# Rotary scores of a latent attention: the low keys' product over 128 partitions instead of 64

## Chip, cores and metric

One core of one Trainium2 chip runs the whole program. The metric is the device time of one execution in microseconds (us). Before the change three runs took 2120.97, 2120.96 and 2120.81 us; the median is 2120.96 us.

## What is computed

A trunk of two layers over 256 tokens of 2048 features. Each layer is a token mixer and a gated channel mixer, with a norm before and after each. The change lies in the second layer's mixer, an attention with low-rank queries, keys and values and a rotary part that all 16 heads share on the side of the keys. Cut from the reference:

```python
q = (rms_norm(c_q, q_a_norm) @ w_uq).reshape(bsz, seq, C_HEADS, C_NOPE_DIM + C_ROPE_DIM)     # 16 heads, 128 + 64
q = jnp.concatenate([q[..., :C_NOPE_DIM], apply_rope(q[..., C_NOPE_DIM:], cos, sin)], axis=-1)
kv = (rms_norm(c_kv, kv_a_norm) @ w_ukv).reshape(bsz, seq, C_HEADS, C_NOPE_DIM + C_V_DIM)
k_nope, v = kv[..., :C_NOPE_DIM], kv[..., C_NOPE_DIM:]
k_rope = apply_rope(k_r[:, :, None, :], cos, sin)                                             # one, for all heads
k = jnp.concatenate([k_nope, jnp.broadcast_to(k_rope, (bsz, seq, C_HEADS, C_ROPE_DIM))], axis=-1)
o = dense_block_attention(q[:, :, :, None, :], k, v, (C_NOPE_DIM + C_ROPE_DIM) ** -0.5)
return o @ w_out
```

So a score is a product over 128 features plus a product over 64 rotary features.

## The kernel before

Every operand of a product is kept as two float32r parts, high and low, and a product is high high + high low + low high. Weights come in chunks of 128 x 1024 numbers: SyncE loads `raw` (L103), ScalarE casts it to `whi` (L117), VectorE subtracts to get `wlo` (L118), three buffers each. TensorE works through the chunks one after another in the two layers' order: mixer 0, channel mixer 0, mixer 1, channel mixer 1. Between two chunks a `tick` lets generators make one step each; softmaxes, transposes and evacuations are such steps and are so woven into the stream of products. The order on each engine is fixed when the program is built.

`mixer1` first makes the two latent tiles `cq` and `ckv` and the rotary keys `kr`. For each of 8 pairs of heads it then takes a chunk for the queries (`proj_pair`, L172 to L174), one for the keys, one for the values, and for every second pair one for the rotary queries, whose parts are turned and copied to `qr` (L833). A head is then one call of `attend`:

- its two blocks of 128 queries each get a sum of products over 256 keys in PSUM, all issued by L471, **five products a block**. Three are over the 128 plain features (`qk`). The fourth and fifth are the rotary ones. `qr` holds the 64 high features of a head on partitions 0 to 63 and the 64 low ones on partitions 64 to 127; `kr[:, 0, :]` holds the high keys twice, on either half. The fourth product, over all 128 partitions, so gives high high and low high at once. The fifth is high high features by low keys: `qr[0:64]` by `kr[0:64, 1, :]`, over 64 partitions.
- VectorE takes the maxima (L480, L482), ScalarE the exponentials (L487) and the high weights (L492), VectorE the low ones (L493). Some ticks later TensorE transposes them (L252), ScalarE copies these to `pT` (L506), and TensorE multiplies by the values.

Heads come in twos, so the products of L471 stand in 8 runs of 20 (the first run has a few others between).

`kr` is made once, by `evac_kr`: two transposes of 64 partitions (L803), the rotary, four transposes back, and one ScalarE copy out of PSUM (L816, 128 x 512), which fills `kr[:, 1, :]` on all 128 partitions too, with the low keys twice.

Ahead of `mixer1` stands the end of the first layer's channel mixer (`out_proj`): the second half of the tokens' products end, ScalarE takes their square sums (L292) and a root (L382), VectorE makes the norm's factor of it (`postv` L383, `postu` L385 and L386, `postr` L387) and adds to the residual x (L391), TensorE transposes x (L413), and its parts (L527, L528) are what mixer 1's first products (L172) wait for.

The lines that say it:

```python
ps = self.psum("at").rearrange("p (i k) -> p i k", i=2)
for i in range(2):
    pairs = scores(i)
    for n, (l, r) in enumerate(pairs):
        self.tc.keep_in_program_order(
            nc.tensor.matmul(ps[:, i, :], l, r, start=n == 0, stop=n == len(pairs) - 1))      # L471
```

Of the kernel before, what the change touches and what calls it, by code (L numbers as in the profile page):

```python
# [9 lines left out]
F32 = mybir.dt.float32  # L10
# [16 lines left out]
HOLD = 3        # chunks of weights kept at the end of an output projection, see proj_tok  # L27
LAGS = 3, 2, 1  # ticks from a softmax to its transposes, from these to the values, from a rotary to its transposes

# columns of the packed vectors  # L30
# [7 lines left out]
class Model:  # L38
    """All products are of operands in two float32r parts, high and low: high high + high low + low high.

    A sublayer's input x is kept as parts of x times the pre-norm's gain, features on the partitions; the norm's
    factor of a token goes in where the products leave PSUM (or into the factors of the scores).
    """
# [14 lines left out]
    def now(self, gen, after=()):  # L58
        """A generator that steps at every tick, once those of `after` have ended."""
        self.soon.append((gen, tuple(after)))  # L60
        return gen

    def later(self, gen, after=()):
        """A generator of the queue, of which a few run at a time."""
        self.bg.append((gen, tuple(after)))
        return gen
# [55 lines left out]
    def behind(self, instructions):  # L122
        """A block whose instructions are issued after these, on their engines."""
        stack = ExitStack()
        for ins in instructions:
            stack.enter_context(self.tc.issue_after(ins.ins))
        return stack

    def weights(self, upto=None):
        """The parts of the next chunk; those after it, before `upto`, get split and loaded."""  # L130
        i = self.at
        if upto is None:
            upto = i + (2 if self.lead else 3)
            self.follow()
        for j in range(i, upto):
            self._split(j)
        for j in range(upto, i + 6):
            self._load(j) if j < upto + 4 else None
        self.at += 1
        return self.made.pop(i)  # L140

    def follow(self):
        """Ahead of a chunk: the tiles of x that it meets, if they aren't there yet."""
        if self.lead and not next(self.lead, False):
            self.lead, self.gate = None, ()

# [4 lines left out]
    def warm(self, n):  # L151
        """Products of zeros, for the array's clock to stay up while its next operands get made."""
        ps = self.psum("acc")
        for _ in range(n):
            self.tc.keep_in_program_order(
                self.nc.tensor.matmul(ps[:, :T], self.zeros[:, :P], self.zeros, start=True, stop=True))

    def acc(self, n):
        """n PSUM banks for sums; evacuations that would still hold them come first."""
        while self.held and sum(k for _, k in self.held) + n > 4:  # L160
            self.finish(self.held.popleft()[0])
        return [self.psum("acc") for _ in range(n)]
# [6 lines left out]
    def mm3(self, ps, lh, ll, rh, rl, start, stop):  # L169
        """ps (+)= l.T @ r of operands in two parts."""  # L170
        mm = self.nc.tensor.matmul
        mm(ps, lh, rh, start=start, stop=False)  # L172
        mm(ps, lh, rl, start=False, stop=False)  # L173
        mm(ps, ll, rh, start=False, stop=stop)  # L174

    def proj_t(self, nk, x, tag):
        """[512 outputs] x [256 tokens], outputs on the partitions: 4 PSUM tiles, their halves to be added."""
        mm = self.nc.tensor.matmul
        out = [self.psum(tag) for _ in range(4)]
        for c in range(nk // 2):  # L180
            hi, lo = self.weights()
            for i in range(4):
                for kk in range(2):
                    k = 2 * c + kk
                    s = slice(kk * 512 + i * P, kk * 512 + (i + 1) * P)
                    mm(out[i], hi[:, s], x(k), start=k == 0, stop=False)  # L186
                    mm(out[i][:, :T], lo[:, s], x(k)[:, :T], start=False, stop=k == nk - 1)  # L187
            self.tick()
        return out

    def proj_tok(self, nk, x, order=None, before={}, hold=0):
        """[256 tokens] x [512 outputs], tokens on the partitions: 2 PSUM tiles.

        The last `hold` chunks are kept for the first half of the tokens to be done before the second.
        """
        out = self.acc(2)
# [26 lines left out]
    def proj_small(self, x, n, nk):  # L223
        """[256 tokens] x [n outputs] of one chunk of weights [128, nk * n], tokens on the partitions."""
# [12 lines left out]
    def proj_pair(self, x):  # L237
        """Two heads of [128 outputs] x [256 tokens] of one chunk, outputs on the partitions."""
# [11 lines left out]
    def turn(self, out, x):  # L250
        """out[f, t] = x[t, f] of a float32r block."""
        self.tc.keep_in_program_order(self.nc.tensor.transpose(out, x, self.ident_r))  # L252

    def joined(self, sp, out, ps):
        """The sum of a proj_t tile's halves."""
        b = sp.tile([P, T], F32, tag="half", name="half", bufs=2)
        self.nc.scalar.copy(b, ps[:, T:])  # L257
        self.nc.vector.tensor_tensor(out=out, in0=ps[:, :T], in1=b, op=ALU.add)
        return out

# [4 lines left out]
    def heron(self, s, v, r):  # L265
        """r = 1 / sqrt(v) from the table's root s, by a step of Heron's rule: 2 s / (s s + v)."""
# [6 lines left out]
    def rstd_over(self, ss, r, n, dim):  # L273
        """Factors of a norm of r * x, r a row's factor, from x's square sums ss [128, 2, n], times r."""
# [19 lines left out]
    def table(self, f, x):  # L294
        """Have the table of f loaded ahead of its use, once x [128, 1] is there."""
        self.nc.scalar.activation(self.spare, x, f)

    def pre_norm(self, sp=None):
        """self.r [128 tokens, 2], and on request self.rb [128, 256 tokens] alike on all partitions; a generator."""
# [29 lines left out]
    def split(self, k, src, pre):  # L329
        """Feature tile k of x, transposed, times the gain as two float32r parts."""  # L330
# [11 lines left out]
    def out_proj(self, nk, parts, post, pre, order=None, before={}):  # L342
        """x += post-norm of the output projection; then x's parts for the next product, or x to DRAM.

        The first half of the tokens ends ahead of the second, so that its part of the norm and of the sum lies
        under products; the parts of x come in pairs of feature tiles, of which the next sublayer's first chunks
        of weights ask (see follow).
        """
# [109 lines left out]
    def attend(self, scores, sc, mask, v, v_gen, put, sp):  # L458
        """scores(i): the (lhsT, rhs) of query block i; sc [128 queries, 2]: factors of the scores, or a number;
        v(j): the parts of [128 keys, 128], there once the generator in v_gen has ended; a generator."""  # L460
# [64 lines left out]
    def parted_by(self, hi, lo, x, r):  # L525
        """The parts of x * r."""
# [4 lines left out]
    def mixed(self, sp):  # L531
        """The attention's outputs in parts, feature tiles."""
# [5 lines left out]
    def turned(self, sp, ps, n, block, tab, put, scale=None):  # L538
        """Rotary of n heads, tokens on the partitions, neighbouring blocks of `block` turned against each other,
        times scale(t) of the rows or scale(t, i) of a head's; the parts, transposed, go to put(i); a generator."""  # L540
# [37 lines left out]
    def first_x(self, sp):  # L578
        """The first parts of x, a pair of tiles ahead of each chunk of weights."""
# [154 lines left out]
    def mixer1(self, pre):  # L734
        nc, tc, a = self.nc, self.tc, self.a
        with tc.tile_pool(name="mix1", bufs=1) as sp:
# [8 lines left out]
            kr = sp.tile([P, 2, T], F32R, name="kr")  # L745

# [23 lines left out]
            def rope(y, z, v, n):  # L770
                """y = rotary of v, [128, 2, n heads, 64]; z is room."""
# [22 lines left out]
            def evac_kr(ps):  # L794
                """The shared rotary keys: high parts on either half of the partitions; low parts too."""
# [20 lines left out]
                nc.scalar.copy(kr, pt.bitcast(F32))  # L816
# [24 lines left out]
            for p in range(8):  # L841
# [21 lines left out]
                def head(h, qk=qk, v=v, qr=qr, v_gen=v_gen):  # L863
                    i = h % 2

                    def scores(b):
# [3 lines left out]
                                (qr[0][:, h % 4, bs], kr[:, 0, :]), (qr[0][0:64, h % 4, bs], kr[0:64, 1, :])]  # L870
# [83 lines left out]
def _tiled(w, n=512):  # L954
    """[K, N] -> [N / n, K * n / 131072, 128, 1024]: a chunk, 1024 / n blocks of rows, is a contiguous piece."""
# [6 lines left out]
def _rope(pos, dim):  # L962
    """Cosines and signed sines, [positions, dim] each, of halves turned against each other."""
# [52 lines left out]
```

## Time and profile before

| | |
|---|---|
| median of three runs | 2120.96 us |
| span of the profiled execution | 2119.2 us |
| TensorE (PE) busy | 2106.1 us, 99% of the span |
| VectorE (DVE) busy | 1331.3 us, 63% |
| ScalarE (ACT) busy | 1140.5 us, 54% |
| chain that ended last | PE 98%, DVE 1%, ACT 1% |
| granted TensorE clock, mean | 0.999 |

The profiled execution's span, from its first to its last instruction, is 2119.2 us, 1.8 us under the median of the runs. A share over the whole span says little about one stage; mixer 1's attention lies between about 1159 and 1291 us, and the rows below are of that stage and of the border ahead of it. PE is counted busy from a product's start to its modelled end, and products overlap, so a pause between two products shows in the distance between their starts and not in the busy time.

### The profile page before, as it was taken

What the parts mean: (1) busy time and instruction counts of PE and PEld (TensorE: products, weight loads), DVE (VectorE), ACT (ScalarE), POOL (GpSimd) and SP (SyncE); (2) the same over time, 40 slices, a digit from 0 to 9 for tenths busy, and PEclk for the clock granted to TensorE, in tenths of its full rate; (3) what the DMA queues carried; (4) which work ended last, traced back from release to release, by engine and by line L of the source; (5) the groups of instructions that cost most, each with busy time, mean ns of one, the idle gap of its engine ahead of it and who ended that gap; (6) DMA issues with size and microseconds to landing.
All of it is one profiled execution on the core that took longest, in us unless ns stands there. A gap on an engine that the chain in (4) does not pass through costs nothing.

```text
span 2119.2 us, 29704 instructions
## 1 busy us (share of the span) xinstructions
PE 2106.1 (99%) x11317; PEld 1787.4 (84%) x11317; DVE 1331.3 (63%) x2004; ACT 1140.5 (54%) x1814; POOL 0.2 (0%) x4
## 2 busy tenths in 40 slices
PE   9999999999999999999999999999999999999998
PEld 7888878888888888888888998788888888888886
DVE  6776657767667666444466764576676766754444
ACT  6766546555555555334355765465555555543433
POOL 0000000000000000000000000000000000000000
PEclk9999999999999999999999999999999999999999
DMA  8545565666666666666655335566666666666664
GB/s 312 170 138 159 167 182 176 182 195 188 191 192 183 195 189 190 191 191 193 194 182 164 102 108 155 169 194 191 190 187 195 184 196 190 185 193 194 194 189 149
DMA packets 108718, 385.99 MB, mean 182 GB/s; under 512 B 12064, under 2 KB 12576, under 8 KB 108576
## 3 DMA queue, kind: packets, MB, share of 16 engines
q1 hardware_dynamic: 108288, 383.83, 60.1%
q8 instruction: 88, 1.44, 0.3%
q14 instruction: 54, 0.44, 0.1%
q10 hardware_dynamic: 288, 0.28, 0.0%
HBM read 381.96 MB, written 2.10 MB: 181 GB/s over the span
## 4 chain that ended last, share of the span: by engine, by line
PE 98%; DVE 1%; ACT 1%; DMA 0%; issue 0%; DVEq 0%; SPq 0%
PE ps L186 31%; PE ps L174 16%; PE ps L172 16%; PE ps L173 16%; PE ps L187 15%; PE ps L471 2%; PE ps L252 2%; DVE x L391 0%; PE ps L413 0%; DMA raw<-in_w_in 0%; ACT whi L117 0%; ACT junk L292 0%; PE ps L789 0%; DVE xhl L528 0%; PE ps L790 0%
## 5 line engine op out<-in xcount | busy, mean ns | idle before, releaser
L118 DVE TENSOR_TENSOR wlo<-raw,whi 128x1024 fp32r<-128x1024 f32 (+1 forms) x710 | 867.1, 1222 | 698.3 <-ACT whi L117 697.6
L117 ACT CAST whi<-raw 128x1024 fp32r<-128x1024 f32 (+1 forms) x710 | 743.8, 1048 | 775.9 <-PE ps L174 421.6
L186 PE MATMUL ps<-xhl,whi 128*128 128x512 f32 x2816 | 978.6, 394 | 1.0 <-DVE xhl L528 1.0
L187 PE MATMUL ps<-xhl,wlo 128*128 128x256 f32 x2816 | 779.1, 277 | 0.0
L186 PEld LDWEIGHTS ps<-xhl,whi 128*128 128x128 f32 x2816 | 527.6, 188 | 123.1 <-DVE xhl L528 2.1
L187 PEld LDWEIGHTS ps<-xhl,wlo 128*128 128x128 f32 x2816 | 528.9, 188 | 1.0 <-DVE wlo L118 0.5
L174 PE MATMUL ps<-whi,gl 128*128 128x512 f32 x704 | 280.9, 399 | 0.0
L173 PE MATMUL ps<-wlo,gh 128*128 128x512 f32 x704 | 277.4, 394 | 0.0
L172 PE MATMUL ps<-whi,gh 128*128 128x512 f32 x704 | 276.0, 392 | 0.0
L173 PEld LDWEIGHTS ps<-wlo,gh 128*128 128x128 f32 x704 | 132.2, 188 | 34.5
L172 PEld LDWEIGHTS ps<-whi,gh 128*128 128x128 f32 x704 | 132.2, 188 | 31.4
L174 PEld LDWEIGHTS ps<-whi,gl 128*128 128x128 f32 x704 | 132.2, 188 | 30.3
L172 PE MATMUL ps<-whi,xhl 128*128 128x512 f32 x352 | 138.5, 395 | 1.5 <-ACT whi L117 1.5
L173 PE MATMUL ps<-wlo,xhl 128*128 128x512 f32 x352 | 137.9, 392 | 0.0
L174 PE MATMUL ps<-whi,xhl 128*128 128x512 f32 x352 | 137.6, 392 | 0.0
L172 PE MATMUL ps<-whi,oh 128*128 128x512 f32 x256 | 101.5, 397 | 0.0
L174 PE MATMUL ps<-whi,ol 128*128 128x512 f32 x256 | 101.4, 396 | 0.0
L173 PE MATMUL ps<-wlo,oh 128*128 128x512 f32 x256 | 100.9, 394 | 0.0
L257 ACT COPY half<-ps 128x256 f32<-128x256 f32 x176 | 65.0, 369 | 45.7 <-PE ps L186 36.0
L172 PEld LDWEIGHTS ps<-whi,xhl 128*128 128x128 f32 x352 | 65.9, 188 | 15.1 <-ACT whi L117 1.7
L174 PEld LDWEIGHTS ps<-whi,xhl 128*128 128x128 f32 x352 | 66.0, 188 | 14.0
L173 PEld LDWEIGHTS ps<-wlo,xhl 128*128 128x128 f32 x352 | 66.1, 188 | 13.3 <-DVE wlo L118 0.9
(177 smaller groups left out, 1722.4 us busy)
## 6 DMA issues: line engine op xcount, KB each, us to landing
raw<-in_w_up SPq DMA_DIRECT2D x352, 512.0 KB, 4.2
raw<-in_w_down SPq DMA_DIRECT2D x176, 512.0 KB, 4.2
raw<-in_w_in SPq DMA_DIRECT2D x88, 512.0 KB, 4.0
raw<-in_w_out SPq DMA_DIRECT2D x64, 512.0 KB, 4.0
gb<-in_post SPq DMA_DIRECT2D x16, 256.0 KB, 4.2
raw<-in_w_qn SPq DMA_DIRECT2D x8, 512.0 KB, 3.6
raw<-in_w_kn SPq DMA_DIRECT2D x8, 512.0 KB, 3.5
raw<-in_w_v SPq DMA_DIRECT2D x8, 512.0 KB, 3.6
```

The costliest lines, as they stand in the source:

```text
L117: self.nc.scalar.copy(hi[:, s], raw[:, s])
L118: self.nc.vector.tensor_tensor(out=lo[:, s], in0=raw[:, s], in1=hi[:, s].bitcast(F32), op=ALU.subtract)
L172: mm(ps, lh, rh, start=start, stop=False)
L173: mm(ps, lh, rl, start=False, stop=False)
L174: mm(ps, ll, rh, start=False, stop=stop)
L186: mm(out[i], hi[:, s], x(k), start=k == 0, stop=False)
L187: mm(out[i][:, :T], lo[:, s], x(k)[:, :T], start=False, stop=k == nk - 1)
L252: self.tc.keep_in_program_order(self.nc.tensor.transpose(out, x, self.ident_r))
L257: self.nc.scalar.copy(b, ps[:, T:])
L471: nc.tensor.matmul(ps[:, i, :], l, r, start=n == 0, stop=n == len(pairs) - 1))
```

## The change

`kr[64:, 1, :]`, the second copy of the low keys, is replaced by zeros: a memset writes them once at the start of `mixer1`, and the copy out of PSUM is split in two so that it leaves them alone. The fifth product then takes `qr` and `kr` on all 128 partitions; its upper half multiplies the low features of the queries by zeros. Comments were also taken out of the file; two lines are added in all, so that lines behind the memset have a number one higher and those behind the copy two higher.

```diff
@@ mixer1
             kr = sp.tile([P, 2, T], F32R, name="kr")
+            nc.vector.memset(kr[64:, 1, :].bitcast(F32), 0.0)
...
@@ evac_kr
-                nc.scalar.copy(kr, pt.bitcast(F32))
+                nc.scalar.copy(kr[:, 0, :], pt[:, 0, :].bitcast(F32))
+                nc.scalar.copy(kr[0:64, 1, :], pt[0:64, 1, :].bitcast(F32))
...
@@ scores
-                                (qr[0][:, h % 4, bs], kr[:, 0, :]), (qr[0][0:64, h % 4, bs], kr[0:64, 1, :])]
+                                (qr[0][:, h % 4, bs], kr[:, 0, :]), (qr[0][:, h % 4, bs], kr[:, 1, :])]
```

TensorE's instructions keep their order and their waits, and so do SyncE's. Two places change on the other engines. The first is VectorE at the end of the first layer's `out_proj`, in the order after the change (`postv` to `postr` are the second half of the tokens' factor, `x` is the residual, in brackets is the engine or queue waited for):

```order
L391 SCALAR_TENSOR_TENSOR x_343<-m_9425,postr,x_343 128x512
L118 TENSOR_TENSOR wlo<-raw,whi 128x1024 [waits DMAHW3_49,Activation_49]
L746 MEMSET kr 64x256 [waits PE_49]
L383 TENSOR_SCALAR postv<-posta,part 128x1 [waits Activation_49]
L385 SCALAR_TENSOR_TENSOR postu<-posts,postv 128x1 [waits DVE_49,Activation_49]
L386 RECIPROCAL postu<-postu 128x1 [waits DVE_49]
L387 TENSOR_SCALAR postr<-posts,postu 128x1 [waits DVE_49]
```

The memset is the only row that is new there; written at the start of `mixer1`, it is placed behind a split of weights and ahead of the factor. The PE instruction that it waits for is the last product of this `out_proj` (L174), since `kr` lies where a tile of the channel mixer lay.

The second place is ScalarE where `kr` is filled (`v` and `qk` are the first heads' evacuations), before:

```order
L522 CAST qk<-ps 128x2x256 [waits PE_49]
L816 CAST kr<-ps 128x512 [waits PE_49]
L117 CAST whi<-raw 128x1024 [waits DMAHW6_49,PE_49,Activation_49]
L522 CAST v<-ps 128x512
L117 CAST whi<-raw 128x1024 [waits DMAHW7_49,PE_49,Activation_49]
```

and after:

```order
L522 CAST qk<-ps 128x2x256 [waits PE_49]
L817 CAST kr<-ps 128x256 [waits PE_49]
L818 CAST kr<-ps 64x256
L117 CAST whi<-raw 128x1024 [waits DMAHW6_49,PE_49,Activation_49]
L522 CAST v<-ps 128x512
```

One copy became two, in the same place.

## Rows read from the trace of the kernel before

**Rows 1.** The page's first line of busy times, and its chain of waits by engine.

```profile
PE 2106.1 (99%) x11317; PEld 1787.4 (84%) x11317; DVE 1331.3 (63%) x2004; ACT 1140.5 (54%) x1814; POOL 0.2 (0%) x4
PE 98%; DVE 1%; ACT 1%; DMA 0%; issue 0%; DVEq 0%; SPq 0%
```

**Rows 2.** The instructions of L471 that read `qk` and `kr`: count, shortest, median and longest time in ns, first and last start in us, and forms (partitions * columns of the array, then the operand's shape). PEld is the load of the operand that stays in the array.

```profile
L471 PE MATMUL ps<-qk x96: 277/282/388, 1159.3 to 1277.4; 128*128 128x256 f32 x96
L471 PEld LDWEIGHTS ps<-kr,qr x64: 182/185/189, 1160.1 to 1277.7; 128*128 128x128 f32 x32, 64*128 64x128 f32 x32
L471 PE MATMUL ps<-kr,qr x64: 276/330/384, 1160.2 to 1277.7; 128*128 128x256 f32 x32, 64*128 64x256 f32 x32
```

**Rows 3.** The timeline of PE and of PEld over one block of scores and the start of the next, from narrow windows: start in us, time in us, engine, line, operation, form, how many were merged.

```profile
1160.71 0.62 PE L471 MATMUL ps<-qk 128*128 128x256 f32 x3
1161.06 0.19 PEld L471 LDWEIGHTS ps<-kr,qr 128*128 128x128 f32 x1
1161.17 0.28 PE L471 MATMUL ps<-kr,qr 128*128 128x256 f32 x1
1161.38 0.18 PEld L471 LDWEIGHTS ps<-kr,qr 64*128 64x128 f32 x1
1161.38 0.38 PE L471 MATMUL ps<-kr,qr 64*128 64x256 f32 x1
1161.69 0.39 PE L471 MATMUL ps<-qk 128*128 128x256 f32 x1
1161.92 0.40 PE L471 MATMUL ps<-qk 128*128 128x256 f32 x2
```

**Rows 4.** The timeline of PE over products of a chunk of weights, of the same shape (17 in a row, of which the first and the last are shown), and over the two transposes of 64 partitions in `evac_kr`.

```profile
1164.01 0.28 PE L172 MATMUL ps<-whi,ckv 128*128 128x256 f32 x1
...
1165.93 0.28 PE L173 MATMUL ps<-wlo,ckv 128*128 128x256 f32 x1
...
1145.78 0.28 PE L174 MATMUL ps<-cq,wlo 128*128 128x256 f32 x1
1145.99 0.34 PE L803 MATMUL ps<-ident,raw 64*128 64x64 f32 x2
1146.25 0.38 PE L172 MATMUL ps<-ckv,whi 128*128 128x256 f32 x1
1146.47 0.28 PE L173 MATMUL ps<-ckv,whi 128*128 128x256 f32 x1
```

**Rows 5.** The chain of waits in order of time, around the fifth run of L471: start, time, engine, tile and line, number of instructions.

```profile
1224.11 3.74 PE ps L471 x20
...
1228.16 0.12 PE ps L173
```

**Rows 6.** The timeline of DVE and ACT, and pieces of the chain of waits, at the border of the two layers. In square brackets is the idle time ahead of an instruction and what ended it.

```profile
1081.45 1.22 DVE L118 TENSOR_TENSOR wlo<-raw,whi 128x1024 fp32r<-128x1024 f32 x1
1082.62 0.21 DVE L383 TENSOR_SCALAR postv<-posta,part 128x1 f32<-128x1 f32 x1
...
1082.62 0.29 ACT L382 ACTIVATE posts<-posta,part 128x1 f32<-128x1 f32 x1
...
1082.95 0.23 DVE postu L385
...
1085.20 0.50 PE ps L172
```

**Rows 7.** The two memsets that the kernel has on DVE (groups of the page's kind: busy us, mean ns of one).

```profile
L928 DVE MEMSET zeros<- 128x128 uint32 x1 | 0.2, 165 | 0.0
L924 DVE MEMSET eps<- 128x1 f32 x1 | 0.1, 59 | 0.8 <-PEq L1008 0.8
```

**Rows 8.** The timeline of ACT at the copy to `kr` and behind it, and the summary of another copy out of PSUM, of 128 x 256 (L518).

```profile
1152.45 0.59 ACT L816 CAST kr<-ps 128x512 fp32r<-128x512 f32 x1 [1.23 <-PE ps L252]
1152.93 1.05 ACT L117 CAST whi<-raw 128x1024 fp32r<-128x1024 f32 x1
1155.62 1.05 ACT L117 CAST whi<-raw 128x1024 fp32r<-128x1024 f32 x1 [1.15 <-issue]
...
L518 ACT CAST oh<-ps x32: 349/368/423, 89.0 to 1296.3; 128x256 fp32r<-128x256 f32 x32
```

**Rows 9.** The timeline of DVE and ACT at the first two heads' softmax, and of PE where the last of their weights get transposed.

```profile
1160.97 0.69 DVE L523 TENSOR_TENSOR qk<-ps,qk 128x512 fp32r<-128x512 f32 x1 [0.23 <-ACT qk L522]
1161.80 0.69 DVE L480 TENSOR_REDUCE nm<-ps 128x2 f32<-128x512 f32 x1
1163.77 0.69 DVE L480 TENSOR_REDUCE nm<-ps 128x2 f32<-128x512 f32 x1 [1.28 <-PE ps L471]
1164.61 1.28 ACT L487 ACT_TABLE_LOAD   x1 [3.68 <-DVE nm L482]
...
1171.68 0.28 PE L173 MATMUL ps<-cq,whi 128*128 128x256 f32 x1
1171.85 0.28 PE L252 MATMUL ps<-ident_r,phl 128*128 128x128 f32 x1
```

**Rows 10.** Busy time of the engines in the stretch from the second run of L471 to the third: window, its length, then busy us and instructions of each engine, granted clock, DMA's busy share and GB/s. Under it, from the summary of L471, what PE sat idle for ahead of it: us in all, times.

```profile
1172.77:1189.63 16.86, 16.86 (x137) 15.80 (x137) 12.43 (x23) 13.04 (x30) 0.00 (x0) 1.00 0.42 125
...
  ACT pT L506: 0.7, 3
```

## Prediction

> **What bounds the kernel now.** I read the page's first lines, then L471 by itself, then single instructions, then the neighbours that could take over. The page says that TensorE is busy 99% of the span and makes up 98% of the chain that ended last [rows 1]. So a microsecond taken out of TensorE's stream counts in full, as long as what feeds it keeps up, and one added beside it counts nothing. Busy time does not show where that stream stands still, though: products overlap, so I go by the distance of their starts.
>
> The summary of L471 shows a difference of form: the products by `kr` have a median of 330 ns against 282 ns of those by `qk`, and half of them, 32, are over 64 partitions [rows 2]. The timeline of one block shows what that does [rows 3]. The fourth product, over 128 partitions, starts at 1161.17 and its load had started at 1161.06, under the products before it. The fifth, over 64, starts at 1161.38 and its load starts only then. The next block's first product, again over 128, starts at 1161.69, its second at 1161.92. So the three distances from the fourth product on are 0.21, 0.31 and 0.23 us, 0.75 us in all. Products of the same shape whose partitions stay at 128 stand (1165.93 - 1164.01) / 16 = 0.12 us apart [rows 4], three of them 0.36 us. **A block loses 0.75 - 0.36 = 0.39 us around its fifth product.**
>
> That it is the change of 64 and 128 partitions, and not the tiles `qr` and `kr`, is supported by the only other place with 64 partitions, the two transposes at L803 [rows 4]: 0.21 us from the last full product to the first of them, and 0.22 us from the first full product behind them to the next, as here, with other tiles and another operation. The fourth product reads the same two tiles as the fifth and follows its predecessor without a pause.
>
> A rule of the Trainium skill speaks against this change: in "TensorE: Matmul & The Clock Gate", section "LDWEIGHTS (loading the stationary operand)", a load's time is set by its columns, and "A 32×128 weight load takes the same time as a 128×128 weight load". The trace agrees for the load's own time, 182 to 189 ns over both forms [rows 2]. By that rule alone widening the product to 128 partitions would gain nothing, and the sum would be 2121.2 us; it is the start of the load that differs in the rows, and on that the rule says nothing. It is rival D below.
>
> **The change part by part.**
>
> *The fifth product over 128 partitions.* Each of the 32 blocks has one. The column count is unchanged, so the product itself gets no longer than a neighbour of 0.12 us. If the pauses at both borders go, 32 x 0.39 = 12.5 us. The same from a whole run: 20 products of L471 and the one behind take 1228.16 - 1224.11 = 4.05 us in the chain [rows 5], where 21 at 0.12 would take 2.52; 1.53 us a run, for 8 runs 12.2 us. The two differ by rounding; I take 12.3. It lies on the chain, in full. Its bounds: 12.5 above; below, nothing, if the pauses have another cause.
>
> *The memset.* It is not on TensorE's stream but it isn't free either. It stands on VectorE ahead of `postv`, and waits for the last product of that sublayer, which ACT's square sums wait for as well, so the wait itself adds none. But VectorE isn't idle there: the split `wlo` runs from 1081.45 for 1.22 us and `postv` follows it at once, at 1082.62 [rows 6]. The memset goes between. Its price: 165 ns for 128 columns of 4 bytes, 59 ns for one [rows 7]; for 256 columns that extends to 59 + 255 x (165 - 59) / 127 = 272 ns (an estimate from these two rows). `postv` would end at about 1082.62 + 0.27 + 0.21 = 1083.10 instead of 1082.83; `postu`, which today waits for ACT's root (1082.62 + 0.29 = 1082.91) and starts at 1082.95, would start some 0.15 to 0.2 us later. From there everything up to mixer 1's first product at 1085.20 is on the chain [rows 6]. I take **+0.2 us**; bounds 0 (the split ends earlier than it shows) and 0.3.
>
> *The split copy to `kr`.* One copy of 128x512 takes 0.59 us, the next starts 0.48 us after it [rows 8]; two of 256 columns would take some 0.37 us each [rows 8], so ACT gets 0.15 to 0.25 us more. It delays the split of weights behind it, and behind that ACT is idle for 1.15 us [rows 8], which takes it up; the first use of `kr` is at 1160.2 [rows 2], 7 us later. I put **+0.1 us** for what VectorE passes on before; bounds 0 and 0.25. Were that idle time gone, the whole 0.25 would show.
>
> *What a shorter run triggers.* Scores that end sooner let the softmax start sooner, but the transposes behind it also come sooner. In the later runs the chain is released by the scores' end, so both move. The first run is the tight one: VectorE waited 1.28 us for the second head's scores before the reduction at 1163.77, so this can move by that and by the 0.14 us that the first reduction can move up to the end of the subtraction ahead of it (1160.97 + 0.69 = 1161.66 against 1161.80) [rows 9], 1.42 of the 1.53 us. ACT, idle for 3.68 us before the table load at 1164.61, follows. PE already waits a little at the end of that softmax: the transpose at 1171.85 starts 0.17 us after the product ahead [rows 9]. So **+0.1 us** is given back there; bounds 0 and the run's whole 1.53. Late next are the transposes' copies to `pT`, for which PE idles 0.7 us in three times [rows 10]; they follow the transposes on the same engine and stay as they are.
>
> *What feeds TensorE.* The stretch from the second run to the third has ACT at 13.04 of 16.86 us and VectorE at 12.43 [rows 10]. With 1.53 us less it is 15.33 us, and ACT is at 85%, VectorE at 81%. DMA's share of 0.42 there becomes 0.46. All of them still fit.
>
> **The sum:** -12.3 + 0.2 + 0.1 + 0.1 = **-11.9 us**. Against the profiled execution, 2119.2 us of span, that is 2107.3; its median of runs lies 1.8 us above the span, so I forecast **2109.1 us**. By the bounds of the terms that are likely (gain 12.2 to 12.5, additions 0 to 2.1 us) the time lies between 2108.5 and 2110.9.
>
> **The rivals.**
>
> *A, the forecast*, 2109.1 us: 0.85.
>
> *B, one border stays.* The pause going in (0.21 - 0.12 = 0.09 us a block) could be due to the fourth and fifth product sharing the operand in the array, or to something else that the change leaves. Then 32 x 0.09 = 2.9 us stay: 2112.0 us. Against it: the first and second product of a block share theirs too. From 1160.71 to 1161.17 are three distances, 0.46 us [rows 3]; the first of them is the way out of the block before, 0.23 us as from 1161.69 to 1161.92, and leaves 0.12 us for each of the others, no pause. 0.04.
>
> *C, ACT takes over.* At 85% in the second stretch, with softmaxes that come in twos, ACT could hold the transposes back so that the first run's and one more run's gain turn into waits: 2 x 1.53 = 3.1 us back, 2112.1 us. For it: the tight transpose at 1171.85 [rows 9]. Against it: at the first run VectorE waits 1.28 us for PE, and ACT 3.68 us for VectorE [rows 9]. 0.06.
>
> *D, the slower side.* The pauses come not from the count of partitions but from a switch that stays, say of the pair of tiles. Then nothing is gained, and what decides is the memset ahead of `postv`: from the point where it ends later than ACT's root (1082.91) every part of it is on the chain, and with 0.2 us the time is 2121.2 us, above the time before. To be slower by a measurable amount it would have to take over 4 us, which the 165 ns of the other memset speak against. The rule of the Trainium skill above ends here too ("TensorE: Matmul & The Clock Gate", same section): by that rule, partitions are free. Against D: the pause at L803. 0.04.
>
> *E, the change doesn't do what it says*, for instance because the product built still reads 64 partitions: 2121.2 us with the same additions. The indices in the diff read all 128; 0.01.
>
> **How the numbers follow.** The likeliest case gives 2109.1. Its own range is 2108.5 to 2110.9; with it alone 0.85 is held, and I widen it a little, for rounding and for additions that I haven't seen, to 2108.0 to 2111.4. B to E, 0.15, lie outside. A measurement of this kernel can tell about 0.2%, 4.2 us, from no change. A, B and C are all faster by more than that: 0.95. D and E are within: 0.04 of their 0.05, and I leave 0.01 for a D whose additions cost over 4.2 us.
>
> **What would show it.** In the profile after: all 64 products by `kr` of the form 128*128, with a median near 280 ns; a run of L471 of 20 products in about 2.4 us instead of 3.74; the fifth product's load starting ahead of it, as the fourth's does. The memset stands between `wlo` and `postv` with some 0.27 us, and mixer 1's first product starts about 0.2 us later. The two copies to `kr` take some 0.7 us together. The stage from the first run to the last is shorter by about 11 us (seven runs at 1.53) in step with PE, and PE's idle time in it stays below 1 us. The forecast is wrong if pauses of over 0.05 us remain around the fifth products, if PE gets new waits for `phl` or `pT` of over 1 us, or if time changes outside 1080 to 1300 us.

## The result, and the profile after

Nine runs of each kernel were made beside each other: a median of 2109.01 us after (lowest 2108.62) and 2121.14 us before (lowest 2120.81). The ratio is 0.9938, with a 95% interval of 0.9913 to 0.9962; the two medians alone make 0.9943. The interval is wide because runs of either kernel come at two levels some 9 us apart, before 6 near 2121 and 3 near 2130, after 5 near 2108.8 and 4 near 2117.8, and the ratio takes them all in. From lowest to lowest it is -12.19 us; in the profiled executions the span went from 2119.2 to 2106.8 us, -12.4 us. The forecast was 2109.1 us, with a span of 2107.3.

The page after, busy times and chain, against [rows 1]:

```profile
PE 2093.1 (99%) x11317; PEld 1783.0 (85%) x11317; DVE 1330.9 (63%) x2005; ACT 1139.5 (54%) x1815; POOL 0.2 (0%) x4
PE 98%; DVE 1%; ACT 1%; issue 0%; DMA 0%; DVEq 0%; SPq 0%
```

The count of products is the same; PE's busy time is 13.0 us shorter, since the modelled ends of the products had covered the pauses and so counted them as busy, and PE still makes up the chain.

All instructions on the tile `kr` after (count, shortest/median/longest ns, first and last start us, forms), against [rows 2, 7, 8]:

```profile
L471 PEld LDWEIGHTS ps<-kr,qr x64: 187/188/192, 1160.5 to 1265.5; 128*128 128x128 f32 x64
L471 PE MATMUL ps<-kr,qr x64: 277/280/282, 1160.6 to 1265.6; 128*128 128x256 f32 x64
L746 DVE MEMSET kr<- x1: 272/272/272, 1082.8 to 1082.8; 64x256 f32 x1
L817 ACT CAST kr<-ps x1: 377/377/377, 1152.9 to 1152.9; 128x256 fp32r<-128x256 f32 x1
L818 ACT CAST kr<-ps x1: 368/368/368, 1153.1 to 1153.1; 64x256 fp32r<-64x256 f32 x1
```

All 64 products have one form, and their median fell from 330 to 280 ns. The memset takes the 272 ns that were worked out.

PE and its loads over a block (timeline, narrow windows), against [rows 3]: first the loads of the next block before, then the whole block after.

```profile
1161.69 0.42 PEld L471 LDWEIGHTS ps<-qk 128*128 128x128 f32 x3
```

```profile
1161.09 0.30 PEld L471 LDWEIGHTS ps<-kr,qr 128*128 128x128 f32 x2
1161.20 0.40 PE L471 MATMUL ps<-kr,qr 128*128 128x256 f32 x2
1161.32 0.31 PEld L471 LDWEIGHTS ps<-qk 128*128 128x128 f32 x2
1161.44 0.52 PE L471 MATMUL ps<-qk 128*128 128x256 f32 x3
1161.79 0.40 PE L471 MATMUL ps<-kr,qr 128*128 128x256 f32 x2
```

The fourth and fifth product now go from 1161.20 to 1161.44 and the next three from there to 1161.79, 0.12 us each. The load for the next block starts at 1161.32, ahead of its product, where it used to start with it (both at 1161.69). A whole run, from the chain of waits, against [rows 5]:

```profile
1218.15 2.36 PE ps L471 x20
```

2.36 us instead of 3.74. Comparing the start of every product in the two traces shows the whole account:

| place | PE's shift against before, us |
|---|---|
| up to 1080 us | +0.05 |
| first transposes behind the norm's factor (1084 us) | +0.50 |
| first product of the scores (1160 us) | +0.42 |
| behind the eighth run (1300 us) | -12.36 |
| from 1400 us to the end | -12.40 |

In every block the shift has three steps: 0.09 at the fifth product, 0.19 at the next and 0.11 at the one behind, 0.39 us in all. After the last run nothing moves by more than 0.07 us.

### The profile page after: what moved, and what is told of

Read it like the earlier page. It is cut to its first block, busy times and chain, and to the rows that moved or that the text cites. A ratio compares the mean times of both kernels' runs of the same rounds, so it can differ in the third digit from the quotient of the medians.

```text
span 2106.8 us, 29706 instructions
## 1 busy us (share of the span) xinstructions
PE 2093.1 (99%) x11317; PEld 1783.0 (85%) x11317; DVE 1330.9 (63%) x2005; ACT 1139.5 (54%) x1815; POOL 0.2 (0%) x4
## 4 chain that ended last, share of the span: by engine, by line
PE 98%; DVE 1%; ACT 1%; issue 0%; DMA 0%; DVEq 0%; SPq 0%
PE ps L186 31%; PE ps L174 16%; PE ps L172 16%; PE ps L173 16%; PE ps L187 15%; PE ps L252 2%; PE ps L471 2%; DVE x L391 0%; PE ps L413 0%; DMA raw<-in_w_in 0%; ACT whi L117 0%; ACT junk L292 0%; PE ps L790 0%; DVE wlo L118 0%; DVE xhl L528 0%
## 5 line engine op out<-in xcount | busy, mean ns | idle before, releaser
L186 PE MATMUL ps<-xhl,whi 128*128 128x512 f32 x2816 | 978.6, 394 | 1.0 <-DVE xhl L528 1.0
L187 PE MATMUL ps<-xhl,wlo 128*128 128x256 f32 x2816 | 779.2, 277 | 0.0
L186 PEld LDWEIGHTS ps<-xhl,whi 128*128 128x128 f32 x2816 | 527.6, 188 | 123.0 <-DVE xhl L528 2.0
L187 PEld LDWEIGHTS ps<-xhl,wlo 128*128 128x128 f32 x2816 | 528.9, 188 | 1.1 <-DVE wlo L118 0.6
L174 PE MATMUL ps<-whi,gl 128*128 128x512 f32 x704 | 280.9, 399 | 0.0
L174 PEld LDWEIGHTS ps<-whi,gl 128*128 128x128 f32 x704 | 132.2, 188 | 30.4
L174 PE MATMUL ps<-whi,xhl 128*128 128x512 f32 x352 | 137.6, 392 | 0.0
L174 PE MATMUL ps<-whi,ol 128*128 128x512 f32 x256 | 100.9, 394 | 0.0
L174 PEld LDWEIGHTS ps<-whi,xhl 128*128 128x128 f32 x352 | 66.0, 188 | 14.0
```

## The experiments

The times of each stand against runs of the kernel before that were made beside it, the starts of its products against the one trace of the kernel before. Where a profile fell on the upper level of times, only its part up to 1360 us is compared; the last section says why.

**The change once more**, without an edit.

> The changed kernel once more, as the yardstick for the others of this chip. It takes out the pauses (0.394 us a block, 32 blocks, 12.6 us) and adds the memset ahead of the norm's factor (0.44 us by the shift of the first transposes behind it). Expected span 2106.8 us, lowest run 2108.6 us, 12.2 us under the lowest run before. If the difference of 12.2 us was of the one chip, it would be off by over 1 us here.

Five runs took 2108.52, 2108.53, 2108.62, 2108.74 and 2117.54 us, against a lowest of 2120.43 before: -11.9 us. (A sixth took 6584.21 us; nothing shows why, and it is set aside.) The profiled run is the one of 2117.54, and its span is 2115.7. The difference came again within 0.3 us of the first.

**All 128 partitions without zeros.** The low keys' second copy is left where it was:

```diff
-                                (qr[0][:, h % 4, bs], kr[:, 0, :]), (qr[0][0:64, h % 4, bs], kr[0:64, 1, :])]
+                                (qr[0][:, h % 4, bs], kr[:, 0, :]), (qr[0][:, h % 4, bs], kr[:, 1, :])]
```

> The kernel before with one edit: the fifth product reads all 128 partitions of both tiles, and the upper half of the low keys stays the second copy that was there. It so adds the product of the low features and low keys, which the kernel before leaves out. No memset, no split copy. Theory (the pauses come from the borders between products over 64 and over 128 partitions; the memset costs 0.44 us on the chain at the end of the first layer): 32 products of full height, no pause, and 0.4 us less than the change: span 2106.4 us, lowest run 2108.2 us. Rival (it is the zeros that make the product quick): pauses stay or come back in part, over 2110 us. Rival (the 0.44 us is made up later by something else): 2108.6 us, as the change.

Products of `kr` in its trace (summary of the tile), and VectorE at the border of the layers (timeline), against [rows 6]:

```profile
L471 PEld LDWEIGHTS ps<-kr,qr x64: 187/188/192, 1159.8 to 1264.9; 128*128 128x128 f32 x64
L471 PE MATMUL ps<-kr,qr x64: 277/280/282, 1159.9 to 1265.0; 128*128 128x256 f32 x64
```

```profile
1081.27 1.22 DVE L118 TENSOR_TENSOR wlo<-raw,whi 128x1024 fp32r<-128x1024 f32 x1
1082.44 0.21 DVE L383 TENSOR_SCALAR postv<-posta,part 128x1 f32<-128x1 f32 x1
1082.77 0.22 DVE L385 SCALAR_TENSOR_TENSOR postu<-posts,postv 128x1 f32<-128x1 f32 x1
```

The pauses are gone without any zeros, and `postv` follows the split at once again. Between 1040 and 1360 us PE gains 12.87 us on the kernel before, the change 12.41: the additions cost the difference, 0.46 us. So the zeros are not what makes the product quick. The lowest run is 2108.09 us, as the theory had it. But 10 of its 12 runs took 2116.8 to 2118.2 us, and the median is 2116.94 (ratio 0.997, 0.9957 to 0.9982): it is no better version of the whole program as it stands.

**Half as many borders.** In the second block of a head the order of the five products is turned round, so that two products over 64 partitions follow each other:

```diff
-                        return [(qt[:, 0, bs], kt[:, 0, :]), (qt[:, 0, bs], kt[:, 1, :]), (qt[:, 1, bs], kt[:, 0, :]),
+                        pairs = [(qt[:, 0, bs], kt[:, 0, :]), (qt[:, 0, bs], kt[:, 1, :]), (qt[:, 1, bs], kt[:, 0, :]),
                                 (qr[0][:, h % 4, bs], kr[:, 0, :]), (qr[0][0:64, h % 4, bs], kr[0:64, 1, :])]
+                        return pairs if b == 0 else pairs[::-1]
```

> The kernel before, the order of the products turned round in the second block of each head: the fifth product of the first block, over 64 partitions, is followed by that of the second block, also over 64. So there are 16 pairs and 32 borders instead of 64; nothing else moves. Theory (each border between 64 and 128 partitions costs, not the product itself): the second of a pair starts about 0.12 us after the first, and 16 x 0.39 = 6.3 us go; span 2112.9 us. Rival (every product over 64 partitions pauses, wherever it stands): 2119.2 us, as before, with distances of 0.2 to 0.3 us between the two of a pair. Rival (the pause sits between the fourth product and the fifth because these two read the same operand in the array): also as before.

One run, 2114.72 us, with a span of 2112.9, just what the theory said; by its second channel mixer it lies on the lower level (346.7 ns a pair of products there, see the last section). The timeline of PE over one pair, from narrow windows (merged rows overlap; the first row of `kr` is the first block's fourth product, then the two over 64 partitions, the second block's fourth, and the three by `qk`):

```profile
1160.31 0.28 PE L471 MATMUL ps<-kr,qr 128*128 128x256 f32 x1
1160.51 0.81 PE L471 MATMUL ps<-kr,qr 64*128 64x256 f32 x3
1160.74 0.59 PE L471 MATMUL ps<-kr,qr 64*128 64x256 f32 x2
1160.94 0.38 PE L471 MATMUL ps<-kr,qr 128*128 128x256 f32 x1
1161.16 0.52 PE L471 MATMUL ps<-qk 128*128 128x256 f32 x3
```

The distances are 0.20, 0.23, 0.20 and 0.22 us, against four of 0.117: 0.39 us lost for the pair, where two products apart lost that much each. The second product over 64 partitions does not start 0.12 us after the first, as I had written, but 0.23, inside the 0.2 to 0.3 us of the rival; it is the span, 6.3 us shorter, that speaks against the rival. The four distances fit this: **each border costs 0.09 us at the first product behind it and 0.11 us at the second**, 0.19 to 0.20 us in all. Before, the product between two borders had both at once, 0.12 + 0.11 + 0.09, the 0.31 us of [rows 3]. So the rival of a pause that belongs to every product over 64 partitions falls, since there are as many of them as before and half the loss is gone. That of a pause between two products that read the same operand in the array falls too: such neighbours are as many as before, and with 128 partitions the fourth and fifth still share theirs and stand 0.12 us apart. Three or more products over 64 in a row were not run.

**96 partitions.** The kernel before, its fifth product with `0:96` in the place of `0:64`:

```diff
-                                (qr[0][:, h % 4, bs], kr[:, 0, :]), (qr[0][0:64, h % 4, bs], kr[0:64, 1, :])]
+                                (qr[0][:, h % 4, bs], kr[:, 0, :]), (qr[0][0:96, h % 4, bs], kr[0:96, 1, :])]
```

> The kernel before, the fifth product over 96 partitions instead of 64 (it adds 32 of the low features by the low keys, which the kernel before leaves out). In the built program a product over 64 partitions asks for an array of 64 x 128, one over 96 for the whole 128 x 128, as one over 128 does. Theory 1 (the pause comes with the change of the array's form, 64 x 128 against 128 x 128): no pause, span 2106.4 us. Theory 2 (the pause comes with any change of the count of partitions): pauses of 0.39 us a block stay, span 2119.2 us.

```profile
L471 PEld LDWEIGHTS ps<-kr,qr x64: 187/188/192, 1159.5 to 1264.6; 128*128 128x128 f32 x32, 96*128 96x128 f32 x32
L471 PE MATMUL ps<-kr,qr x64: 276/281/287, 1159.6 to 1264.7; 128*128 128x256 f32 x32, 96*128 96x256 f32 x32
```

In this summary of `kr`, half of the products are over 96 partitions, and the median is 281 ns. PE gains 12.80 us between 1040 and 1360 us, against 12.87 with 128. So the count of partitions may change without a pause, and theory 2 falls. Theory 1 fits: what costs is the change between the array's 64 x 128 form, which the built program asks for with 64 partitions, and its whole 128 x 128. That the program asks for the whole array with 96 is read from the program; the trace prints 96\*128. Only 64, 96 and 128 were run. (The run took 2116.68 us, its profile on the upper level.)

**The additions alone.** The change, with the fifth product over 64 partitions:

```diff
-                                (qr[0][:, h % 4, bs], kr[:, 0, :]), (qr[0][:, h % 4, bs], kr[:, 1, :])]
+                                (qr[0][:, h % 4, bs], kr[:, 0, :]), (qr[0][0:64, h % 4, bs], kr[0:64, 1, :])]
```

> The change without its gain: memset and split copy as in it, the fifth product over 64 partitions as before. Theory (the memset holds back the norm's factor by 0.44 us, the split copy costs nothing): all pauses there, TensorE 0.44 us later than before from the first transposes behind the factor on and no more than that at the first scores; span 2119.7 us. Rival (the forecast's sizes, memset 0.2 us and copy 0.1 us): 2119.5 us, with a step of 0.2 us at the border of the layers and another of 0.1 us at about 1160 us.

One run of 2121.59 us, with a span of 2119.8; by the starts of PE it is 0.55 us behind the kernel before from 1200 us to the end. 0.45 us come in one step, at the first transposes behind the factor. The other 0.13 us come between 1120 and 1200 us, in steps of 0.06 and 0.07. They could be the split copy's, but that isn't shown: the run with half as many borders has no split copy and moves by 0.05 us between 1120 and 1160 us as well, and in the change itself nothing is seen of it.

**The memset on POOL.**

```diff
-            nc.vector.memset(kr[64:, 1, :].bitcast(F32), 0.0)
+            nc.gpsimd.memset(kr[64:, 1, :].bitcast(F32), 0.0)
```

> The change with its memset on the POOL engine instead of VectorE; the same sums. Theory (the 0.44 us is the memset's place in VectorE's line, ahead of the factor): they come back, the norm's factor ends as early as before the change; span 2106.4 us, lowest run 2108.2 us, in the rhythm of products that the change's first profile shows in the second channel mixer. Rival (a memset anywhere at that time costs, since it waits for the same last product and writes beside VectorE): 2106.8 us, lowest 2108.6 us. In the other rhythm of products, which two profiles showed, either is 8.9 us longer.

POOL's timeline, then VectorE's:

```profile
1081.84 0.31 POOL L746 MEMSET kr<- 64x256 f32 x1 [1081.40 <-PE ps L174]
```

```profile
1081.37 1.22 DVE L118 TENSOR_TENSOR wlo<-raw,whi 128x1024 fp32r<-128x1024 f32 x1
1082.54 0.21 DVE L383 TENSOR_SCALAR postv<-posta,part 128x1 f32<-128x1 f32 x1
1082.86 0.22 DVE L385 SCALAR_TENSOR_TENSOR postu<-posts,postv 128x1 f32<-128x1 f32 x1
```

The same memset on another engine, where it starts a microsecond sooner, costs the factor nothing: PE gains 12.87 us between 1040 and 1360 us. Runs took 2108.22, 2108.26, 2108.44, 2117.06, 2117.24 and 2117.24 us; against the change's lowest of 2108.52 in another set of runs that is 0.3 us, which agrees with the 0.46 us but wouldn't show it by itself.

**A product of zeros in the second channel mixer.** On the version with 128 partitions and no zeros, once, ahead of the second half of the sixth group:

```diff
+                if layer == 1 and gi == 5:
+                    ps = self.psum("at")
+                    self.tc.keep_in_program_order(
+                        nc.tensor.matmul(ps[:, :T], self.zeros[:, :P], self.zeros, start=True, stop=True))
                 pv = self.proj_t(KD, x, "at")
```

> The kernel in which the fifth product also takes the low features by the low keys, with one more product, of zeros, in the second channel mixer, between the two halves of its sixth group of eleven. In two profiles the products of that mixer ran in a rhythm of three pairs, 349, 350 and 361 ns, in the others of two, 350 and 343 ns, from the same place on to the end of that stage. Theory (the rhythm is a matter of how the train of products is started, and stays until it is broken): after the extra product the rhythm can differ from that ahead of it within one run, and times between 2108.2 and 2117.0 us occur, near 2112.9 us where it changes. Rival (it is a property of the whole run, of memory or of the chip): the same rhythm ahead and behind, times at 2108.4 and 2117.2 us only.

Nine of ten runs took 2116.92 to 2118.24 us, and one 2113.04, a time that neither of the two levels has and that is near the 2112.9 of a rhythm that changes half way. The profile is of a run of 2117.13 us and has the same rhythm ahead and behind. One run supports the theory; it does not settle it.

**Another order of the channel mixers' products.** On the same version:

```diff
+                s = [slice(kk * 512 + i * P, kk * 512 + (i + 1) * P) for kk in range(2)]
                 for kk in range(2):
-                    k = 2 * c + kk
-                    s = slice(kk * 512 + i * P, kk * 512 + (i + 1) * P)
-                    mm(out[i], hi[:, s], x(k), start=k == 0, stop=False)
-                    mm(out[i][:, :T], lo[:, s], x(k)[:, :T], start=False, stop=k == nk - 1)
+                    mm(out[i], hi[:, s[kk]], x(2 * c + kk), start=c + kk == 0, stop=False)
+                for kk in range(2):
+                    mm(out[i][:, :T], lo[:, s[kk]], x(2 * c + kk)[:, :T], start=False, stop=2 * c + kk == nk - 1)
```

> The kernel in which the fifth product also takes the low features by the low keys, with another order in both channel mixers' first products: two products over 512 columns and then two over 256, where they alternated. Sums and counts are the same. Theory (the two rhythms, 346.7 and 353.3 ns a pair, come from the alternation of 512 and 256 columns): one rhythm only, runs within 1 us of each other, at about 2108.2 us if four products still take 693 ns; 22 groups of 64 pairs make each ns a pair worth 1.4 us a layer. Rival (the rhythms don't depend on the order in the pair): two levels of times again, 2108.2 and 2117.0 us.

Five runs took 2113.08 to 2113.32 us: one level, as the theory said, but 5 us above the lower one. In the second channel mixer a pair takes 348.3 ns here, against 346.7 and 353.3 in the two rhythms.

## Where the prediction was right, and which steps failed

- **Where TensorE stands still.** Right. The pause came with the change between 64 and 128 partitions; it went at both ends (rival B is out), and loads start ahead of their products again. It is not the number of partitions as such: 96 among 128 cost nothing. The array's form fits all the runs. The argument from L803 was sound.
- **The rule that a load's time does not hang on its partitions** (the Trainium skill, "TensorE: Matmul & The Clock Gate", section "LDWEIGHTS (loading the stationary operand)"). It holds here for the load's own time, 182 to 192 ns in any form. What rival D drew from it, no gain and 2121.2 us, did not come: the change of form costs 0.19 to 0.20 us a border.
- **The gain, 12.3 us. This step failed in size:** 12.87 us with nothing added, above the 12.5 that the forecast gave as its upper bound. Three distances were set against 0.12 us, read from a chunk's products; in a run of L471 a product takes 2.36 / 20 = 0.118 us, and the three steps are 0.394 us a block, 12.6 us. Of the remaining 0.25 us, 0.08 come ahead of the first scores, where the version without zeros has no edit that could act, and so are no part of the gain; the others are small steps inside the stage, whose cause was not traced.
- **The memset, 0.2 us. This step failed in size too:** it cost 0.45, above its bound of 0.3. I let the 0.27 us start where `postv` had started and gave `postu` a slack of 0.12 us. The chain of waits after shows both wrong:

```profile
1081.58 1.14 DVE wlo L118
1082.72 0.11 issue
1082.83 0.27 DVE kr L746
1083.10 0.03 issue
1083.13 0.22 DVE postv L383
1083.36 0.03 issue
1083.38 0.02 DVEq L385
1083.40 0.04 issue
1083.45 0.23 DVE postu L385
...
1085.69 0.50 PE ps L172
```

  The memset starts 0.11 us behind the split's end (0.11 also in the second trace of the change and in that of the additions alone), where `postv` had started 0.05 us ahead of it [rows 6], and `postu` starts 0.09 us after the end of `postv` in this chain, so 0.03 us of slack were left, not 0.12. 0.11 + 0.05 + 0.27 + 0.03 - 0.03 makes 0.43.
- **The split copy, 0.1 us.** The change shows none: PE's shift is +0.50 at the factor and +0.42 at the first scores. The two copies and the split behind them cost ACT some 0.06 us (0.54 us to the next start, 0.48 before [rows 8]). ACT's idle time behind takes it:

```profile
1152.86 0.38 ACT L817 CAST kr<-ps 128x256 fp32r<-128x256 f32 x1 [1.23 <-PE ps L252]
1153.13 0.37 ACT L818 CAST kr<-ps 64x256 fp32r<-64x256 f32 x1
1153.40 1.06 ACT L117 CAST whi<-raw 128x1024 fp32r<-128x1024 f32 x1
1156.03 1.06 ACT L117 CAST whi<-raw 128x1024 fp32r<-128x1024 f32 x1 [1.10 <-issue]
```

- **The first run's softmax, 0.1 us.** Right in kind. The two reductions now follow each other without the 1.28 us between them [rows 9], the table load moved from 1164.61 to 1163.65 and from a shift of +0.42 to one of -0.96, 1.38 us, near the 1.42 worked out. PE's shift behind that run was -1.16 us and is -1.13 at the last transposes of that softmax: 0.03 us was given back.

```profile
1161.99 1.51 DVE L480 TENSOR_REDUCE nm<-ps 128x2 f32<-128x512 f32 x2
1163.42 0.29 DVE L482 TENSOR_SCALAR nm<-nm 128x2 f32<-128x2 f32 x2
```

- **ACT as the next bound (rival C).** It did not come. The stretch from the second run to the third has ACT at 13.21 of 15.31 us, 86%, and PE's idle time ahead of L471 for `pT` is what it was [rows 10]:

```profile
1171.61:1186.92 15.31, 15.31 (x138) 15.31 (x137) 12.27 (x23) 13.21 (x30) 0.00 (x0) 1.00 0.44 136
```

```profile
  ACT pT L506: 0.7, 3
```

- **The sum.** -12.87 + 0.46 = -12.41 us in the trace, where the forecast had -11.9. The gain was forecast 0.6 us too small and the memset 0.25 us too small, which work in opposite directions, and the 0.1 us each for the copy and the softmax did not come. On the lower level the time is so still inside the range: the lowest run is 2108.62 us and the median 2109.01, a tenth of a microsecond from the forecast, which is in part luck, since this median is the highest of its level.
- **The range, 2108.0 to 2111.4 us. This step failed as well.** The ratio times the median given before the change makes 0.9938 x 2120.96 = 2107.8 us, 0.2 us under the low end; the ratio of the medians, 0.9943, would make 2108.8. The sum's 0.5 us, of the mis-sized gain above all, used up half of the 1.1 us of room at the low end, and a ratio over runs at two levels did the rest: its interval alone spans 2102.5 to 2112.9 us. The four upper runs lie 6 us over the high end. The forecast put the spread between the levels at nothing: the three runs shown before all lay on the lower one, and I took their spread for the kernel's. One of its own signs of being wrong, a change of time outside 1080 to 1300 us, holds for the upper runs: 8.9 us between 1390 and 1860 us.

## What to carry to other kernels

In a stream of products on TensorE, look at the distance of their starts wherever the form of the array changes: a single product over 64 partitions among those over 128 cost two borders, 0.39 us, three times the 0.12 us of a product, and filling it up, with zeros or with data that are there anyway, cost the stream nothing in this stage (other data than zeros add a term to the sum). Two products over 64 next to each other cost what one alone did. And when an instruction is put in front of a chain that waits, price it with the gap in front of it, or give it to an engine that has nothing in that chain.

## What the runs showed of the hardware that was not expected

**Two rhythms of one train of products.** The upper level of times comes from one place: between 1390 and 1860 us, the first products of the second channel mixer (L186 and L187, 512 and 256 columns in turn). The shift between a lower and an upper profile of the changed kernel is 0 up to 1390 us, grows by 0.77 us in every 40 us, and stays at 8.9 us from 1880 us on. Two windows of each, the change's first profile and then its second (columns as in [rows 10]):

```profile
1440.00:1480.00 40.00, 40.00 (x233) 35.01 (x232) 25.96 (x42) 20.55 (x31) 0.00 (x0) 1.00 0.64 193
1480.00:1520.00 40.00, 40.00 (x232) 34.99 (x232) 26.41 (x41) 19.98 (x30) 0.00 (x0) 1.00 0.62 190
```

```profile
1440.00:1480.00 40.00, 40.00 (x229) 34.72 (x228) 25.12 (x38) 19.78 (x30) 0.00 (x0) 1.00 0.63 193
1480.00:1520.00 40.00, 40.00 (x228) 34.69 (x227) 25.83 (x41) 19.95 (x29) 0.00 (x0) 1.00 0.62 186
```

PE is busy all the time and at a granted clock of 1.00, the upper of its two levels (2.4 GHz), in both, but gets through four products fewer in 40 us. Pairs take 350 and 343 ns by turns in the one, and 361, 349 and 350 in the other, on average 346.7 and 353.3 ns; over the 1333 pairs of that stretch the 6.7 ns make 8.9 us. The rhythm is there from the stage's first undisturbed products and holds to its end. The first channel mixer has the faster one in all the profiles with the products in this order. The kernel before has runs at both levels too, but no trace of an upper one, so for it the place isn't shown. How often the upper level comes differs between kernels: in 5 of 50 runs of the kernel before, in 5 of 14 of the changed one, and in 10 of 12 of that without zeros, beside 2 of 17 of the kernel before. So a part of the gain can be lost there, on average over the runs. What sets the rhythm, and its frequency, is open. The slower one did not come when the two lengths were grouped by twos, in five runs.

**Borders are paid in two instalments**, 0.09 us at the first product behind and 0.11 at the second, and add up in one distance where two borders meet.
